# Add and GELU over 1024 x 4096: y loaded in three pieces in place of four, the adds dealt anew

## The chip, the core and the metric

One core of one Trainium2 chip. The metric is the device time of one execution in microseconds, the median of several; lower is better. A profile is taken of one further execution.

## The reference

```python
def reference(x, y):          # both 1024 x 4096, float32
    z = x + y
    return 0.5 * z * (1 + tanh(sqrt(2 / pi) * (z + 0.044715 * z ** 3)))
```

33.55 MB are read and 16.78 MB written.

## The kernel before

Eight rows of the input stand in each of the 128 partitions: 32768 columns. x is loaded into a tile z that holds everything and is worked on in place; y goes through two tiles of 8192 columns, so the third and fourth loads of y must wait until earlier columns have been added. A chunk is 2048 columns. z and y lie in SBUF, the core's on-chip memory. Each chunk takes four steps on three engines: an add (VectorE or GpSimd), the magnitude and the GELU of its negative (ScalarE, into PSUM, a second on-chip memory), and a close on VectorE, max(z, 0) + GELU(-|z|), which is the result.

```python
    YS = 8192; CH = 2048; PS = 2
    xloads = [16384, 16384]
    yloads = [8192, 8192, 8192, 8192]
    FIRST = 8
    stores = [16384, 10240, 6144]
    # chunk -> the close ahead of which VectorE's queue has this add; the other adds are GpSimd's
    by_dve = {0: 0, 2: 0, 4: 2, 6: 4, 8: 8, 12: 10}
    ...
    sp = [(load_y, 0), (load_x, 0), (load_y, 1), (load_x, 1), (load_y, 2), (load_y, 3)]
    sp += [(store, i) for i in range(len(stores))]
    pool = [(add, c) for c in range(C) if c not in by_dve]
    for c in range(C):
        dve += [(add, k) for k in sorted(by_dve) if by_dve[k] == c] + [(end, c)]
        acts += [(mag, c), (gelu, c)]
```

Each engine is given its instructions as one queue, and in the traces a ready instruction stands behind one that waits (VectorE's idle 4.12 us, below). All transfers are issued on one queue, in the order of `sp`, and are carried out by 16 DMA engines. A store waits for the close of the last chunk that it covers.

## Time and profile before

| | before |
|---|---|
| time, median | 120.04 us (3 runs) |
| span of the profiled run | 118.6 us |
| DMA share of the span | 98.6% |
| VectorE, ScalarE, GpSimd busy | 50%, 51%, 47% |
| second store issued | 96.34 us |

The groups of the page, by line, engine, operation and shape, with busy time, mean duration in ns, idle time before them and what ended it:

```profile
L149 POOL TENSOR_TENSOR z<-z,y 128x2048 f32<-128x2048 f32 x10 | 55.3, 5563 | 45.6 <-DMA z<-in_x_dram 31.1
L166 DVE SCALAR_TENSOR_TENSOR z<-z,w 128x2048 f32<-128x2048 f32 (+1 forms) x17 | 36.4, 2157 | 16.0 <-ACT w L157 16.0
L149 DVE TENSOR_TENSOR z<-z,y 128x2048 f32<-128x2048 f32 x6 | 24.0, 4009 | 30.3 <-DMA z<-in_x_dram 30.1
```

L149 is the add, on either engine; its means of 5.6 and 4.0 us include waiting for one another. L166 is the close.

### The profile page before, as it was taken

The numbers are of one execution on the slowest core, as the hardware profiler recorded it, in microseconds if no ns is written. First come the engines' busy times: TensorE is split into PE (matmuls) and PEld (weight loads), VectorE is DVE, ScalarE is ACT, GpSimd is POOL, SyncE is SP. The second block draws the span as 40 slices with busy tenths as digits, with TensorE's granted clock in tenths as the row PEclk, the third lists the DMA queues.
The fourth block names the chain that finished last, engine by engine and source line by source line (L and its number), as shares of the span: only waits on it lengthen the run. The fifth ranks groups of instructions, "written<-read, shape, count | busy, mean of one in ns | idle before, by whom it ended". The sixth has DMA issues, their size and how long they took to land.

```text
span 118.6 us, 160 instructions
## 1 busy us (share of the span) xinstructions
DVE 59.8 (50%) x24; ACT 60.8 (51%) x34; POOL 55.5 (47%) x14
## 2 busy tenths in 40 slices
DVE  0000000000399999699994594257999457742000
ACT  5000000000067979999379705797798999940000
POOL 0000000000399999997000029999999999100000
DMA  7989888998889988988899898998899889999996
GB/s 243 464 365 696 354 354 354 663 398 354 354 387 497 531 354 354 707 354 354 354 420 464 365 520 354 531 531 354 354 531 531 354 354 442 442 442 442 398 398 265
DMA packets 1296, 50.33 MB, mean 424 GB/s; under 512 B 144, under 2 KB 144, under 8 KB 144
## 3 DMA queue, kind: packets, MB, share of 16 engines
q1 hardware_dynamic: 1296, 50.33, 98.6%
HBM read 33.55 MB, written 16.78 MB: 424 GB/s over the span
## 4 chain that ended last, share of the span: by engine, by line
DMA 48%; POOL 34%; POOLq 4%; ACT 3%; DVE 2%; issue 0%; SPq 0%; DVEq 0%
POOL z L149 34%; DMA z<-in_x_dram 26%; DMA y<-in_y_dram 21%; POOLq L213 4%; DVE z L166 2%; ACT w L154 2%; ACT w L157 2%; SPq L132 0%; POOLq L149 0%; DVEq L166 0%
## 5 line engine op out<-in xcount | busy, mean ns | idle before, releaser
L149 POOL TENSOR_TENSOR z<-z,y 128x2048 f32<-128x2048 f32 x10 | 55.3, 5563 | 45.6 <-DMA z<-in_x_dram 31.1
L154 ACT ACTIVATE w<-z 128x2048 f32<-128x2048 f32 x16 | 30.1, 1880 | 42.5 <-DVE z L149 36.0
L166 DVE SCALAR_TENSOR_TENSOR z<-z,w 128x2048 f32<-128x2048 f32 (+1 forms) x17 | 36.4, 2157 | 16.0 <-ACT w L157 16.0
L149 DVE TENSOR_TENSOR z<-z,y 128x2048 f32<-128x2048 f32 x6 | 24.0, 4009 | 30.3 <-DMA z<-in_x_dram 30.1
L157 ACT ACTIVATE w<-w 128x2048 f32<-128x2048 f32 x16 | 29.8, 1862 | 0.5
L198 ACT ACT_TABLE_LOAD x1 | 1.3, 1283 | 1.3 <-PEq L230 1.3
L197 DVE MEMSET one<- 128x1 f32 x1 | 0.1, 59 | 1.3 <-PEq L230 1.3
L198 ACT ACTIVATE one<-one 128x1 f32<-128x1 f32 x1 | 0.2, 203 | 0.0
L230 POOL MEMSET const-float32-0.0<- 128x1 f32 x1 | 0.1, 98 | 0.2 <-issue 0.2
L230 POOL MEMSET const-bfloat16-1.0<- 128x1 bf16 x1 | 0.1, 101 | 0.0
L230 POOL MEMSET const-uint8-127<- 128x1 uint8 x1 | 0.1, 101 | 0.0
L230 POOL MEMSET const-float32-1.0<- 128x1 f32 x1 | 0.1, 98 | 0.0
## 6 DMA issues: line engine op xcount, KB each, us to landing
y<-in_y_dram SPq DMA_DIRECT2D x4, 4096.0 KB, 23.7
out_dram<-z SPq DMA_DIRECT2D x1, 5120.0 KB, 14.9
out_dram<-z SPq DMA_DIRECT2D x1, 3072.0 KB, 11.0
z<-in_x_dram SPq DMA_DIRECT2D x2, 44.9
out_dram<-z SPq DMA_DIRECT2D x1, 21.6
```

The costliest lines, as they stand in the source:

```text
L149: eng.tensor_add(out=zt[:, a:b], in0=zt[:, a:b], in1=yt[s][:, o : o + b - a])
L154: nc.scalar.activation(out=wt[c], in_=zt[:, a:b], func=act.Abs)
L157: nc.scalar.activation(out=wt[c], in_=wt[c], func=act.Gelu_apprx_tanh, scale=-1.0)
L166: ins = nc.vector.scalar_tensor_tensor(out=zt[:, a + o : a + o + n], in0=zt[:, a + o : a + o + n], scalar=0.0, in1=wt[c][:, o : o + n], op ...
L197: nc.vector.memset(one, 0.0)
L198: nc.scalar.activation(out=one, in_=one, func=act.Gelu_apprx_tanh)
L213: tc.compile()
L230: nc = _bacc.Bacc("TRN2", target_bir_lowering=False, num_devices=1)
```

## The change

Its intent: fewer and larger loads of y, with the third in place of the first columns of one larger tile; VectorE and GpSimd no longer fight for their shared port. A chunk boundary is put where the third load begins (column 20416), which makes a narrow chunk of 64 columns and turns chunk numbers from 10 on up by one.

```diff
-    YS = 8192
+    YS = 20416
-    yloads = [8192, 8192, 8192, 8192]
-    FIRST = 8
+    yloads = [8192, 12224, 12352]
+    FIRST = 9
-    xr, yr, sr, cr = (ranges(r) for r in (xloads, yloads, stores, [CH] * (TOT // CH)))
+    xr, yr, sr, cr = (ranges(r) for r in (xloads, yloads, stores, [CH] * 9 + [CH - 64, 64] + [CH] * 6))
-    by_dve = {0: 0, 2: 0, 4: 2, 6: 4, 8: 8, 12: 10}
+    by_dve = {0: 0, 2: 0, 4: 3, 6: 5, 10: 9, 11: 11, 12: 11, 14: 12, 16: 14}
+    turn = {1: 0, 13: 12, 15: 14}
...
+        if c in turn:
+            tc.add_manual_dep(ins.ins, adds[turn[c]].name, ...,
+                reason="the two engines take turns on their shared port")
...
-        store: lambda i: [(end, c) for c in over(cr, *sr[i])] + [(end, FIRST)],
+        store: lambda i: [(end, c) for c in over(cr, *sr[i])] + [(gelu, FIRST)],
```

(Cut: the first store now waits for the first half of a GELU, which is split in two, in place of half a close.)

## The prediction

> **What bounds the kernel now.** I read the page first, then the DMA queue's own waits, then the timeline of single stretches. On the page:
>
> ```profile
> span 118.6 us, 160 instructions
> DMA  7989888998889988988899898998899889999996
> q1 hardware_dynamic: 1296, 50.33, 98.6%
> DMA 48%; POOL 34%; POOLq 4%; ACT 3%; DVE 2%; issue 0%; SPq 0%; DVEq 0%
> ```
>
> The 16 DMA engines are busy for 98.6% of the span: 116.9 us of 118.6. Of the other 1.6 us, about 1.0 us lies before the first packet and 0.5 us after the last. The chain (last line) gives GpSimd 34%, but that is only the path followed back through the compute engines; while it adds, the queue goes on moving. So the kernel is bound by its 50.33 MB, and no compute engine can make it faster, only slower, by letting the queue run dry. What must be read is therefore how early each transfer joins the queue. The DMA issues, in the timeline of the sync engine:
>
> ```profile
> 44.68 0.33 SPq L132 DMA_DIRECT2D y<-in_y_dram  x1
> 57.94 0.33 SPq L132 DMA_DIRECT2D y<-in_y_dram  x1
> 77.61 0.35 SPq L136 DMA_DIRECT2D out_dram<-z  x1
> 96.34 0.34 SPq L136 DMA_DIRECT2D out_dram<-z  x1
> 107.56 0.33 SPq L136 DMA_DIRECT2D out_dram<-z  x1
> ```
>
> With the times from issue to landing (y: 12.0 to 39.8 us, x: 30.9 and 58.8, out: 21.6, 14.9, 11.0) the landings are y0 12.0, x0 31.35, y1 41.1, x1 60.4, y2 70.15, y3 79.85, and the stores 99.2, 111.25 and 118.55. The steps between them are 9.7 us for a load of 32 KB rows, 19.3 for 64 KB rows, 12.1 for 40 KB and 7.3 for 24 KB: proportional to bytes, without a gap. The engines run out of a transfer's packets about 0.5 to 0.8 us before it lands (the packets of the second store begin between 98.35 and 98.7, while the first lands at 99.2). So the margins are: first store issued at 77.61 for engines that come free from 79.07 on, 1.5 us; second store 96.34 for 98.35, 2.0 us; third 107.56 for 110.5, 2.9 us. These are the quantities that the change moves.
>
> The adds, by line, take 5563 ns on GpSimd and 4009 on VectorE on average, but single ones differ:
>
> ```profile
> 31.45 8.80 DVE L149 TENSOR_TENSOR z<-z,y 128x2048 f32<-128x2048 f32 x2 [30.06 <-DMA z<-in_x_dram]
> 31.49 6.61 POOL L149 TENSOR_TENSOR z<-z,y 128x2048 f32<-128x2048 f32 x1 [31.06 <-DMA z<-in_x_dram]
> 33.66 6.59 DVE L149 TENSOR_TENSOR z<-z,y 128x2048 f32<-128x2048 f32 x1
> 93.90 1.88 ACT L154 ACTIVATE w<-z 128x2048 f32<-128x2048 f32 x1
> 94.02 2.29 DVE L166 SCALAR_TENSOR_TENSOR z<-z,w 128x2048 f32<-128x2048 f32 x1 [1.64 <-ACT w L157]
> 95.81 1.86 ACT L157 ACTIVATE w<-w 128x2048 f32<-128x2048 f32 x1
> 97.58 1.88 ACT L154 ACTIVATE w<-z 128x2048 f32<-128x2048 f32 x1
> ```
>
> Alone, an add takes 2.29 us on VectorE and 4.50 on GpSimd. Here GpSimd's add waits 2.2 us for VectorE's first, and VectorE's second waits until GpSimd is through at 38.1, then works for 2.2. A chunk costs ScalarE 1.88 + 1.86, started every 3.68 us (93.90 to 97.58); the closing operation costs VectorE 2.29.
>
> **What the Trainium skill says.** "SBUF — State Buffer", Who interferes with whom: a VectorE instruction with two SBUF inputs and a GpSimd instruction that reads SBUF exclude each other for a whole instruction. The trace agrees (6.6 us in place of 4.5, and 6.6 in place of 2.3). "VectorE: DVE Perf Modes", the section on the TRN2 errata: an fp32 add of N columns takes (N+151)/0.96 ns; for 2048 that is 2.29 us, which the trace has, and for the new 64-column chunk 0.22 us, an estimate. "DMA: Bandwidth & Descriptors", Latency and other measured facts: about 0.6 us from a hardware-generated DMA to its first byte. In this trace the first packet starts 1.02 us after the first issue begins, 0.64 after it ends, which agrees if its 0.38 us are counted apart.
>
> **The change, part by part.**
>
> Loads. Four y loads become three, 32, 48.9 and 49.4 KB rows in place of four times 32. The bytes are the same. Per engine 32 row packets become 24. From the steps of 9.7 and 19.3 us, a 64 KB row takes twice a 32 KB row to within a few ns, so eight fewer packets and one fewer completion are worth 0 to 0.08 us; I take 0.03. New landings: y0 12.0 and x0 31.35 as before; y1 31.35 + 9.7 x 12224/8192 = 45.85; x1 + 19.35 = 65.2; y2 + 14.6 = 79.8; first store as before, engines free from 98.35 on. The floor does not move.
>
> Does y2 join in time? It overwrites columns used by adds 0 to 6. First add 0 and add 2 run back to back on VectorE (31.45 to 35.95), GpSimd does 1 and 3 until 40.4 and 44.85. ScalarE: chunk 1 from 40.4 to 44.2, chunk 2 to 47.85; VectorE closes chunk 2 at 50.15. GpSimd adds chunk 5 on y1's landing, 45.95 to 50.45. VectorE comes to add 4 at 50.1, waits until 50.45, ends at 52.6; chunk 4 leaves ScalarE at 56.4, is closed by 58.7, then add 6 runs to 60.9. y2 is issued at 60.9, engines come free from 64.4: 3.5 us of margin. In time.
>
> The first store. GpSimd adds chunks 8 and 9 from x1's landing: 65.3, 69.85, 74.2. ScalarE's magnitude of chunk 9 (1984 columns) ends at 76.05, the first half of the GELU about 1.0 us later; the store is issued at 77.1 for engines free from 79.05: 1.95 us in place of 1.5. In time.
>
> The second store. It needs chunks up to 13 (column 26624), and 11, 12 and 13 lie wholly in the last load. In the old kernel the last load brought only chunks 12 to 15, so the store waited for one chunk of it; now it waits for three. From y2's landing at 79.8: VectorE starts the 64-column add at 79.9 (0.24), then closes chunk 9 (1984 columns, 2.2) and 10 (0.24), both queued before add 11, then add 11: 79.9 + 0.24 + 2.2 + 0.24 + 2.29, less about 0.08 overlap at each of three joints, gives 84.65. ScalarE: three chunks at 3.68 from 84.7, the last ends at 84.7 + 2 x 3.68 + 3.77 = 95.8. Add 12 ends at 86.9 and add 13 on GpSimd at 91.4, neither in the way. VectorE closes chunk 13 from 95.9 to 98.2. **The second store is issued at about 98.25**, in place of 96.34, while the engines come free from 98.35 to 98.65. That is 0.1 us of margin where the first packet needs about 1.0. So the queue should run dry, for the first time, for 0.6 to 1.3 us: 98.25 + 1.0 = 99.25 against a mean of 98.55 for the first packets, more for the last engines, since at the start of the program the sixteen first packets began over 0.9 us. I take 0.85.
>
> The third store. Add 14 on VectorE waits for GpSimd and ends at 93.6, chunk 16 is added on VectorE by 100.4; ScalarE runs chunks 14, 15 and 16 from 95.75 to 106.9, the last close ends at 109.2. The second store's engines come free near 111.4. In time.
>
> Sum: -0.03 + 0.85 on 120.04 is 120.86; I say 120.85.
>
> **The rivals.** First, **nothing moves**: the restart is quicker than at program start, or end 13 comes half a microsecond earlier, and the time is 120.0 (119.95 to 120.15). For it: all first transfers of later DMAs in this trace follow without a gap with 1.5 us of margin, so the true need is known only to be under 1.5. Against it: 0.1 us is far below anything that this trace shows. Second, **y2 comes late**: if GpSimd's add 5 ended before VectorE asked at 50.1, GpSimd would take the port for add 7 and add 4 would end at 56.7; the chain behind it then puts y2's issue at 65.0, and the queue stands another 1.5 us, giving about 122.4. It needs an error of 0.35 us in my walk. Third, **the gain is real**: larger rows move faster, 119.9. The old trace's 64 KB rows are not faster per byte by more than 0.2%, so it can't be more than 0.1 us. Fourth, the restart is as slow as the program's start, where the first packets took up to twice their usual time; then the gap is 1.5 us and the time 121.5.
>
> **Range and chances.** A quarter of the weight lies on a gap under 0.5 us, most on 0.6 to 1.3, a little on two gaps. The range of 8 in 10 is 120.0 to 121.7. Faster by 2% would be 117.6, under the time of the bytes alone: 0.01. Slower by 2% is 122.4, only with both gaps: 0.05. The rest, 0.94, is within 2%.
>
> **What would show it.** Right: DMA share of the span falls to about 98%, with one gap, near 98.5 to 99.5, and y2's landing within 0.1 us of 79.8; the second store's issue at 98.2; VectorE's first two adds 2.29 us each, without a wait; GpSimd's adds 4.5 us nearly throughout. Wrong: the second store issued before 97.3 with no gap (then my walk from y2's landing is off), or issued at 98.2 and still no gap (then a transfer needs less lead than I think), or a gap at 64.5 (y2 late), or a changed packet time of the 48 KB rows.

## More of the kernel before

The spread is not small beside the effects: eleven runs of the kernel before, in one set of rounds, went from 119.99 to 120.64 us.

## The result, and the profile after

The changed kernel took **120.67 us** in the median (120.52 to 121.04, six runs), the kernel before in the same rounds 120.11. The ratio is 1.005, with a 95% interval of 1.0035 to 1.0065. Ratios here are the mean time of one kernel's runs over that of the other's of the same rounds, so not quite the ratio of the medians. The change makes the kernel slower by half a microsecond: within 2%, but clear of the scatter.

The lines of the page that answer to those shown of before:

```profile
span 119.2 us, 160 instructions
DMA  7989888988969989988896969998998889999796
q1 hardware_dynamic: 1152, 50.33, 98.3%
DMA 42%; ACT 26%; DVE 14%; POOL 5%; issue 4%; SPq 0%; DVEq 0%
L154 POOL TENSOR_TENSOR z<-z,y 128x2048 f32<-128x2048 f32 (+1 forms) x8 | 39.9, 5004 | 58.0 <-DVE z L154 48.6
L183 DVE SCALAR_TENSOR_TENSOR z<-z,w 128x2048 f32<-128x2048 f32 (+2 forms) x17 | 36.6, 2159 | 18.8 <-ACT w L176 18.7
L154 DVE TENSOR_TENSOR z<-z,y 128x2048 f32<-128x2048 f32 (+1 forms) x9 | 19.2, 2149 | 34.2 <-DMA z<-in_x_dram 30.1
```

The packets fell from 1296 to 1152 for the same bytes. The adds cost less on both engines: VectorE's from 24.0 to 19.2 us for nine in place of six, GpSimd's from 55.3 to 39.9 for eight in place of ten. So the compute side became cheaper, and the time rose: the engines were not the bound. The chain that ended last now has ScalarE with 26% in place of 3%, and the "issue" part rose from 0 to 4%; followed in order of time, 19.7 of its 30.9 us on ScalarE lie after the last load's landing, so the stores behind that load are the place to look. The timeline of the sync engine tells what (start, duration, what is issued):

```profile
60.97 0.33 SPq L137 DMA_DIRECT2D y<-in_y_dram  x1
77.01 0.35 SPq L141 DMA_DIRECT2D out_dram<-z  x1
98.37 0.34 SPq L141 DMA_DIRECT2D out_dram<-z  x1
109.45 0.33 SPq L141 DMA_DIRECT2D out_dram<-z  x1
```

The second store goes out at 98.37 in place of 96.34. In the kernel before, the DMA view of the stretch from 98.3 to 98.7 us shows the first store ending and the second beginning together:

```profile
DMA packets 32, 0.66 MB, mean 1639 GB/s; under 512 B 16, under 2 KB 16, under 8 KB 16
```

Sixteen of these packets are completions (under 512 B), one for each engine; the other sixteen are the second store's first rows of 40 KB. In the changed kernel it takes two stretches to find them, 98.4 to 99.1 and 99.1 to 99.5:

```profile
DMA packets 16, 0.00 MB, mean 0 GB/s; under 512 B 16, under 2 KB 16, under 8 KB 16
...
DMA packets 16, 0.66 MB, mean 1638 GB/s; under 512 B 0, under 2 KB 0, under 8 KB 0
```

Between them lies the gap. Packet by packet, the trace has the engines done with the first store from 98.50 to 99.03 us (mean 98.64), and the second store's first packets from 99.21 to 99.36 (mean 99.27): **0.63 us of idle per engine**. Before, the same change-over took 0.01. And why the store is late, on VectorE (the close is L183, the add L154) and ScalarE:

```profile
80.09 0.23 DVE L154 TENSOR_TENSOR z<-z,y 128x64 f32<-128x64 f32 x1 [4.12 <-DMA y<-in_y_dram]
80.23 2.35 DVE L183 SCALAR_TENSOR_TENSOR z<-z,w 128x1984 f32<-128x1984 f32 x2
82.50 4.49 DVE L154 TENSOR_TENSOR z<-z,y 128x2048 f32<-128x2048 f32 x2
...
93.65 4.69 DVE L183 SCALAR_TENSOR_TENSOR z<-z,w 128x2048 f32<-128x2048 f32 x2
94.09 1.86 ACT L176 ACTIVATE w<-w 128x2048 f32<-128x2048 f32 x1
98.37 0.34 SPq L141 DMA_DIRECT2D out_dram<-z  x1
```

VectorE stands idle for 4.12 us before the last load lands. The close of chunk 9, which needs nothing of that load, is ready for the last 2.1 us of this (its GELU ends at 78.01), but it is queued behind the 64-column add that waits for the load. Only after the closes of chunks 9 and 10 does VectorE add chunk 11, at 82.5. From there ScalarE needs three chunks, ending at 95.95, and the close of chunk 13 (the second of the two at 93.65) ends at 98.34.

### The profile page after: what moved, and what is told of

It reads as the page before. It is cut to its first block, busy times and chain, and to the rows that moved or that the text cites. A ratio compares the mean times of both kernels' runs of the same rounds, so it can differ in the third digit from the quotient of the medians.

```text
span 119.2 us, 160 instructions
## 1 busy us (share of the span) xinstructions
DVE 55.0 (46%) x27; ACT 61.1 (51%) x37; POOL 40.1 (34%) x12
## 2 busy tenths in 40 slices
DMA packets 1152, 50.33 MB, mean 422 GB/s; under 512 B 128, under 2 KB 128, under 8 KB 128
## 3 DMA queue, kind: packets, MB, share of 16 engines
q1 hardware_dynamic: 1152, 50.33, 98.3%
## 4 chain that ended last, share of the span: by engine, by line
DMA 42%; ACT 26%; DVE 14%; POOL 5%; issue 4%; SPq 0%; DVEq 0%
DMA z<-in_x_dram 26%; DMA y<-in_y_dram 16%; ACT w L169 14%; ACT w L176 12%; DVE z L154 8%; DVE z L183 6%; POOL z L154 5%; SPq L137 0%; DVEq L154 0%
## 5 line engine op out<-in xcount | busy, mean ns | idle before, releaser
L154 POOL TENSOR_TENSOR z<-z,y 128x2048 f32<-128x2048 f32 (+1 forms) x8 | 39.9, 5004 | 58.0 <-DVE z L154 48.6
L169 ACT ACTIVATE w<-z 128x2048 f32<-128x2048 f32 (+2 forms) x17 | 30.2, 1779 | 44.1 <-DVE z L154 39.4
L183 DVE SCALAR_TENSOR_TENSOR z<-z,w 128x2048 f32<-128x2048 f32 (+2 forms) x17 | 36.6, 2159 | 18.8 <-ACT w L176 18.7
L154 DVE TENSOR_TENSOR z<-z,y 128x2048 f32<-128x2048 f32 (+1 forms) x9 | 19.2, 2149 | 34.2 <-DMA z<-in_x_dram 30.1
L176 ACT ACTIVATE w<-w 128x2048 f32<-128x2048 f32 (+2 forms) x18 | 30.1, 1672 | 0.6
## 6 DMA issues: line engine op xcount, KB each, us to landing
y<-in_y_dram SPq DMA_DIRECT2D x1, 6176.0 KB, 19.1
```

What stands on the lines that cost most here:

```text
L154: ins = eng.tensor_add(out=zt[:, a:b], in0=zt[:, a:b], in1=yt[:, o : o + b - a])
L169: nc.scalar.activation(out=wt[c], in_=zt[:, a:b], func=act.Abs)
L176: ins = nc.scalar.activation(out=w, in_=w, func=act.Gelu_apprx_tanh, scale=-1.0)
L183: nc.vector.scalar_tensor_tensor(out=zt[:, a:b], in0=zt[:, a:b], scalar=0.0, in1=wt[c], op0=alu.max, op1=alu.add,)
```

## The experiments

Twelve runs were made; all gave the right result. "Gap" is the mean over the engines between the last packet of the first store and the first of the second, from the trace's packets. "Before" is the kernel before in the same rounds.

| run | second store issued | gap | time, median | before | ratio (95%) |
|---|---|---|---|---|---|
| the change | 98.37 | 0.63 | 120.67 | 120.11 | 1.0050 (1.0035 to 1.0065) |
| after_again | 98.34 | 0.54 | 120.61 | 120.08 | 1.0038 (1.0026 to 1.0051) |
| e1_close_first | 96.54 | 0.01 | 120.33 | 120.11 | 1.0014 (0.9996 to 1.0031) |
| e1_again | 96.64 | 0.01 | 120.18 | 120.08 | 1.0002 (0.9988 to 1.0016) |
| e2_later_store | 102.64 | 5.03 | 124.92 | 120.11 | 1.0397 (1.037 to 1.0424) |
| e3_no_turns | 103.00 | 5.36 | 125.40 | 120.11 | 1.0437 (1.041 to 1.0464) |
| e4_four_loads | 96.21 | 0.01 | 120.08 | 120.11 | 1.0016 (0.9983 to 1.0048) |
| e4_again | 96.25 | 0.01 | 120.53 | 120.11 | 1.0040 (1.0007 to 1.0074) |
| e5_lead_one | 97.26 | 0.00 | 120.60 | 120.08 | 1.0038 (1.0025 to 1.0052) |
| e6_lead_half | 97.83 | 0.11 | 120.61 | 120.08 | 1.0042 (1.0026 to 1.0058) |
| e7_early_load | 96.69 | 0.00 | 120.46 | 120.13 | 1.0020 (1.0005 to 1.0035) |
| e8_lead_clean | 97.47 | 0.02 | 120.19 | 120.13 | 1.0013 (0.9994 to 1.0033) |
| e9_more_instructions | 96.42 | 0.00 | 120.51 | 120.13 | 1.0032 (1.0018 to 1.0046) |

**e1_close_first and e1_again: the same kernel with the late store mended.** My theory: the loss is the dry queue at the second store. The rival: the loads themselves cost it. The close of chunk 9 needs nothing of the last load, so it goes ahead of the adds that do:

```diff
-    by_dve = {..., 10: 9, 11: 11, 12: 11, 14: 12, 16: 14}
+    by_dve = {..., 10: 10, 11: 10, 12: 10, 14: 12, 16: 14}
```

> The changed kernel, with VectorE's queue turned round in one place: the close of chunk 9 stands ahead of the adds that wait for the last load, and the adds of chunks 11 and 12 ahead of the close of chunk 10. Theory (the loss is the dry queue at the second store): add 11 ends at 82.6 us in place of 84.8, the second store is issued at about 96.2 in place of 98.37, 2.3 us before the first engine comes free, no gap is left, and the time is 119.95 to 120.15, a ratio to the kernel before of 0.999 to 1.001. Rival A (48 KB rows or the three loads themselves cost the half microsecond): the time stays at 120.5 to 120.7. Rival B (the restart costs more than the lead explains, and part of the loss is elsewhere): between the two, about 120.3.

The first measurement had a median of 120.33, between the two theories and where rival B had put it, with single runs from 119.98 to 120.59, so I ran it again beside the changed kernel:

> The changed kernel once more, beside the others on one chip. Theory: 120.5 to 120.8, the second store issued at 98.1 to 98.4, its first packets 0.85 to 1.0 us later, and a gap of about 0.6 us.

> The reordered kernel again, since its first measurement had a median of 120.33 with a spread of 0.6 us and did not separate it from either kernel. Its profile had no gap, but one of the 16 DMA engines finished the first load 0.4 us behind the others and stayed behind to the end. Theory (the gap was the loss; what is left is the scatter of the slowest engine, which the kernel before has too): no gap, 119.95 to 120.35, and 0.3 to 0.6 us faster than after_again. Rival (three loads or 48 KB rows cost something): it stays 0.2 us or more above the kernel before.

The repeat of the change gave 120.61, the reordered kernel 120.18 and the kernel before 120.08. The reordered kernel's timeline and the DMA view of 98.6 to 99.2 us in its second profile:

```profile
78.49 2.22 DVE L183 SCALAR_TENSOR_TENSOR z<-z,w 128x1984 f32<-128x1984 f32 x1 [2.13 <-ACT w L176]
80.63 4.62 DVE L154 TENSOR_TENSOR z<-z,y 128x64 f32<-128x64 f32 x3
...
96.64 0.34 SPq L141 DMA_DIRECT2D out_dram<-z  x1
...
DMA packets 32, 0.66 MB, mean 1092 GB/s; under 512 B 16, under 2 KB 16, under 8 KB 16
```

The close of chunk 9 has moved into the idle time, the three adds follow one another, the store is issued 1.7 us earlier, and completions and first rows stand in one stretch again. No gap is left, and 0.43 us of the 0.53 us that separate the two kernels in these rounds are back. (By the first measurement it was 0.34 of 0.56, with the change measured in other rounds.) So the gap is shown to be most of the loss. Whether the last tenth is real is not: the intervals of both measurements include 1.

**e2_later_store: the same cost, eight times as large.** The second store covers one chunk more.

```diff
-    stores = [16384, 10240, 6144]
+    stores = [16384, 12288, 4096]
```

> The changed kernel with the second store widened by one chunk (48 KB rows, the third store 16 KB), so that it waits for chunk 14. In the changed kernel's trace that chunk is closed at 102.74. Theory (each microsecond that the second store comes late is a microsecond of dry queue): first packets near 103.65 where the engines are free at 98.6, a gap of 5.0 in place of 0.6, and the time is 120.67 + 4.4 = 125.0. Rival (the gap is only partly exposed, since later stores catch up): clearly under 124.

It took 124.92 us, 4.25 more than the change, against 4.4 expected. Issue and first packets (103.3 to 103.7 us):

```profile
102.64 0.34 SPq L141 DMA_DIRECT2D out_dram<-z  x1
...
DMA packets 16, 0.79 MB, mean 1966 GB/s; under 512 B 0, under 2 KB 0, under 8 KB 0
```

The gap of 5.03 us raises the time by 4.81 over the kernel before. With e3 (5.36 and 5.29) and the change itself (0.63 and 0.56) that makes three sizes of gap: the time rises by nearly the whole of it, each time by 0.07 to 0.22 us less. What the small rest is, is not shown. In the profiles the last packet ends 0.78, 5.06 and 5.41 us later than in the kernel before, so no less than the gap, and the span ends 0.38 us after it in place of 0.51.

**e3_no_turns: the waits that make the engines take turns.** The three added waits are taken out (`turn = {}`); no data depends on them.

> The changed kernel without the three added waits that make the two engines take turns. Theory (the port goes to whoever asks first and the queue in the port alternates): on the last load's landing GpSimd adds chunk 13 first, 80.3 to 84.8, VectorE's add 11 waits to 86.9, GpSimd goes on with add 15 until 91.3, VectorE's add 12 ends at 93.5; the second store goes out near 103.4 and the time is about 125.7, 5 us slower than the changed kernel. Rival (the lock alternates anyhow, so the waits are superfluous): within 0.3 us of the changed kernel, 120.4 to 121.0.

125.40 us, against 125.7 expected and 120.67 with the turns. GpSimd's and VectorE's adds after the last load:

```profile
79.89 11.06 POOL L154 TENSOR_TENSOR z<-z,y 128x2048 f32<-128x2048 f32 x2 [5.77 <-DMA y<-in_y_dram]
...
82.25 10.85 DVE L154 TENSOR_TENSOR z<-z,y 128x2048 f32<-128x2048 f32 x2
...
103.00 0.34 SPq L141 DMA_DIRECT2D out_dram<-z  x1
```

Two adds of VectorE took 10.85 us where the change has 4.49. GpSimd takes the port at 79.89 for a chunk that is not wanted yet, and once both ask, they alternate, whole instruction by whole instruction. So within this dealing the turns are worth 4.7 us; the rival, that they are superfluous, falls. They save no transfer time: they keep the wrong chunk from being added first, and the second store from being later still.

**e4_four_loads and e4_again: is it the number of loads?** The kernel of e1 with the last load in two halves, the first of which can be issued at 44.8.

```diff
-    yloads = [8192, 12224, 12352]
+    yloads = [8192, 12224, 6176, 6176]
```

> The kernel of e1_close_first with the last load of y cut into two of 24.7 KB rows, so four loads again. Theory (the transfer time is a matter of bytes; a packet and a completion more cost some ns): the same time as e1_close_first within 0.1 us. Rival (fewer and larger rows are what the change gains): 0.1 to 0.3 us slower than e1_close_first. If the queue had a margin problem at the last load, landing earlier in two halves would show here as a gain, which the theory does not expect, since e1_close_first has no gap.

> The reordered kernel with the last load in two halves, again: its first measurement had one run at 121.18 among six and a median of 120.08. The kernels with three loads and no gap had medians of 120.33, 120.18, 120.46 and 120.19 against 120.11, 120.08, 120.13 and 120.13 of the kernel before. Theory A (three loads cost 0.1 to 0.2 us through slow packets, of which e4's first profile had none): a median of 119.95 to 120.15, no run of slow packets in the profile. Theory B (it is scatter of the transfers, whatever the loads): a median of 120.1 to 120.4 and slow packets among the loads.

The medians were 120.08 and 120.53, 0.25 under and 0.35 over those of e1 in the same order, so both sets missed what was expected of them. In the second set three runs lay from 120.00 to 120.20 and three from 120.86 to 121.26, and one of the first six was at 121.18. Both profiles fell among the quick ones and show no gap and, after the first load, no slow packet among the loads, so what the slow ones are is unknown, and neither theory is confirmed. What stands is that the quick runs of four loads (119.91 to 120.43, picked after the fact) are no slower than those of three or of the kernel before: the larger rows bring nothing that the times can show.

**e5_lead_one, e6_lead_half, e8_lead_clean: how much lead a store needs.** In e5 and e6 the close of chunk 13 is cut into 16 and 24 parts, which delays the store.

```diff
+        for n in [128] * 16 if c == 13 else [b - a]:     # e6: [64] * 16 + [128] * 8
```

> The reordered kernel with the close of chunk 13 cut into 16 parts of 128 columns, so that the second store goes out about 1.0 us later, near 97.2, some 1.2 us before the first engine comes free. Theory (a transfer needs 0.85 us from issue to first packet, and no more): no gap, the time of e1_again within 0.1 us. Rival (a running queue needs the lead of the program's start, 1.0 to 1.9 us): a gap for a part of the engines, 0.2 to 0.6 us slower.

> The same with 24 parts (16 of 64 columns, 8 of 128), so that the second store goes out near 97.85, about 0.55 us before the first engine comes free. Theory: first packets near 98.7 where the engines come free between 98.3 and 98.7, so a gap of 0.1 to 0.4 us by engine; because the last engine to come free sets the end and it waits least, the time rises by 0.0 to 0.25 us over e1_again. Rival (lead as at the program's start): 0.6 us or more.

Both took 120.6, half a microsecond over the kernel before, and so against my expectation. But in the trace e5 has no gap: its store is issued at 97.26, and the packets follow at once from 98.52. e6's store is issued at 97.83, its first packets begin at 98.68, the mean gap is 0.11. The lead was as expected and the time was not, so the cuts must have cost something else. The pages of both have a line that those of all the runs above lack, a packet of 8 KB on the instruction queue; in e6 it comes at 98.6 and a 40 KB packet that starts just after takes 1.87 us in place of 1.51. It looks as if the 15 and 23 added instructions made the core fetch instructions in the middle of the run, on one of the 16 DMA engines. That is not the whole of it: in their profiles the last engine ends only 0.17 us (e5) and 0.33 us (e6) after the next one, and e5's last load also had nine first packets that were 0.05 to 0.35 us too long. So I delayed the store with a single instruction more, starting from e7 (below), by closing 480 columns of chunk 9 before the last load's landing and 1504 after the first add behind it:

> e7_early_load with the close of chunk 9 in two parts, 480 columns before the last load's landing and 1504 after the add of chunk 10, so that the second store goes out near 97.5, 0.8 us before the first engine comes free, with one instruction more instead of the 15 and 23 of e5 and e6, whose profiles show an instruction fetch of 0.35 us on one DMA engine. Theory (0.85 us from issue to first packet is all that a store needs, and e5 and e6 were slow because of the fetch): gaps of at most 0.1 us, no packet on the instruction queue, the time of e7_early_load within 0.1 us. Rival (a store that goes out late costs even without a gap): 0.3 us or more slower than e7_early_load.

```profile
97.47 0.34 SPq L141 DMA_DIRECT2D out_dram<-z  x1
...
DMA packets 32, 0.66 MB, mean 936 GB/s; under 512 B 16, under 2 KB 16, under 8 KB 16
```

The store goes out 0.87 us before the first engine is done (98.34), completions and first rows stand in one stretch (98.2 to 98.9), there is no packet on the instruction queue, and the median is 120.19, faster than its sibling e7 by 0.27 where I had expected at most 0.1. The rival, that a late store costs even without a gap, falls. As to the lead: where the engines stood idle (the change, after_again, e2, e3), the sixteen first packets came 0.84 to 0.99 us after the issue. A lead of 0.87 us just about covers that; it left 0.02 us of gap in the mean and about 0.13 at most. (e6, 0.61 us ahead of the first engine, left 0.11 us.)

**e9_more_instructions: the fetch by itself.** The kernel of e7 with the close of chunk 0, which has much time around it, in 16 parts.

> e7_early_load with the close of chunk 0 cut into 16 parts, long before any store: 15 more VectorE instructions, nothing else moved that a transfer waits for. Theory (the extra instructions make an instruction fetch fall into the run, and it takes one DMA engine 0.35 us): one packet on the instruction queue, one data packet 0.35 us too long, and the time 0.2 to 0.45 us above e7_early_load, since the slowest engine sets the end. Rival (e5 and e6 were slow through the late store): the time of e7_early_load.

The page has the packet again:

```profile
q1 hardware_dynamic: 1152, 50.33, 98.2%
q14 instruction: 1, 0.01, 0.0%
```

The fetch took 0.31 us, from 111.67, and the data packet after it, at 111.98 us, took 0.37 us too long. Fifteen of the engines end by 118.15 us, the one with that packet at 118.71: it alone sets the end. In this profile the fetch put off the end by 0.56 us. The times don't show it as I had expected: 120.51 is 0.32 over e8 but only 0.05 over e7, with which I had said I would compare it, so by that measure the rival's outcome came; e7 was itself slow, with slow packets in its profile. All three kernels with 15 or more added instructions show the fetch and no other does. How much of e5's and e6's half microsecond it is, is not shown.

**e7_early_load: does the last load go out too late?** In the traces with three loads, some first packets of the last load took 0.05 to 0.35 us too long. Its issue, at 61, is 3.5 us before its first packet. I exchanged two adds so that it goes out at 57.

```diff
-    by_dve = {..., 4: 3, 6: 5, ...}
+    by_dve = {..., 4: 3, 7: 6, ...}
```

> The reordered kernel (e1) with chunks 6 and 7 exchanged between the engines: GpSimd adds 6 right after 5, VectorE adds 7 later. The last load, which waits for add 6, should go out near 57.1 in place of 61.2, 7.4 us ahead of its first packets in place of 3.4. Theory (a load issued only 3.4 us ahead starts with slow packets: in all eight runs with three loads some first packets of the last load took 0.05 to 0.35 us too long, in none of the two with four): these packets take their usual 1.825 us, the slowest engine ends the load within 0.45 us of the fastest, and the time falls from about 120.2 to 120.0 to 120.1, level with the kernel before. Rival (scatter, unrelated to when the load is issued): some first packets of the last load are slow here too and the time stays at 120.2 to 120.3.

A miss. The time was 120.46, no lower than e1's. Its first packets were still up to 0.12 us too long, and moreover the 64 KB rows of the second x load took 2.47 us on average in place of 2.42, in nearly all engines. In e8, with the same loads, there was hardly any of that. So when the last load is issued is not what makes these packets slow, or not alone. Such stretches came and went between profiles of nearly the same kernel.

## Why the prediction was right

The time on record was 120.85 and the measured one 120.67, of which 0.56 us are the change against 0.81 foretold (the kernel before read 0.07 us higher in these rounds). Point by point:

- **What bounds the kernel.** Right: cheaper adds bought nothing, and the time moved with the gap in the DMA queue alone, over three sizes of gap.
- **Loads.** The issue of the last load was foretold for 60.9 and came at 60.97, its landing for 79.8 and came at 80.07 (issue and 19.1 us), outside the 0.1 us that the prediction allowed it. The gain of 0.03 us from fewer packets is too small to be seen in the times. By the packets' median durations it is 0.06 us: an engine's y rows take 8 x (1.213 + 1.806 + 1.825) us in place of 32 x 1.213; slow packets outweighed that.
- **First and third store.** Foretold for 77.1 and 109.2, seen at 77.01 and 109.45, both in time.
- **Second store.** Foretold for 98.25, seen at 98.37; e1 shows that this lateness is most of the loss.
- **The size of the gap.** The term that was off: 0.85 us against 0.63. The first packet's mean time was right (99.25 foretold, 99.27 seen). But I had added to it for a start spread over 0.9 us, as at the program's start, and the sixteen first packets began within 0.15 us; and the engines came free at 98.64 in the mean, not at 98.55, in part because first packets of the last load were slow (1.88 us in the mean where 1.825 is usual). The median time then rose by a little less than the gap.
- **The rivals.** "Nothing moves" fell: 0.1 us of margin was too little, and e8 shows that 0.87 would have been all but enough. "y2 comes late" did not happen: add 4 took the port as walked. "The gain is real" fell with e1 and e4, which have no gap and are no faster than the kernel before. The slow restart fell: the second store's first packets took 1.535 us on average, where this size took 1.515 before, and its eight rows lost 0.09 us together. (Nor were the first packets of the program up to twice the usual, as this rival had it: in the trace of before the longest took 2.135 us for 1.213, 1.76 times.)
- **GpSimd's adds** were foretold to take 4.5 us nearly throughout; two of eight took 6.5, waiting on the port.
- The two first adds of VectorE took 2.29 us each without a wait, as foretold; GpSimd's first then waits for both:

```profile
31.47 4.49 DVE L154 TENSOR_TENSOR z<-z,y 128x2048 f32<-128x2048 f32 x2 [30.08 <-DMA z<-in_x_dram]
...
33.84 10.95 POOL L154 TENSOR_TENSOR z<-z,y 128x2048 f32<-128x2048 f32 x2 [33.41 <-DVE z L154]
```

**What stays open.** The kernels without a gap (e8's of 0.02 counted in) had medians of 120.08 to 120.60 against 120.08 to 120.13 of the kernel before. Whether 0.1 us of that belongs to the new loads, why e5 and e7 took 0.3 to 0.5 us more without a gap, and why some runs of e4 took a whole microsecond more, these runs don't settle. No version here beats the kernel before.

## What to carry to other kernels

When the DMA share is 98%, read the margins, not the busy times: for every transfer, how long before the queue runs dry it is issued. A larger last load gives the work behind it less time: here it put three chunks in place of one between that load's landing and the second store, and the margin went from 2 us to 0.1. Look in each in-order queue for work that stands behind a wait it doesn't need; moving one close ahead of the waiting adds, and two adds ahead of another close, took the store 1.7 us forward.

## What the Trainium skill lacked or had wrong

- "DMA: Bandwidth & Descriptors", Latency and other measured facts: the page doesn't say from where its 0.6 us to the first byte are counted; here they fit from the end of the issue (0.50 to 0.65 us for the sixteen engines). From the start of the issue, in the middle of a run, the first packets came after 0.84 to 0.99 us. Nor does it say what lead keeps a running queue from a gap: 1.26 us did, 0.87 left 0.02 us of gap, 0.61 left 0.11, 0.13 left 0.63.
- "SBUF — State Buffer", Who interferes with whom: it says that whoever issues first holds the port for its whole instruction and the other waits. It doesn't say who is next: in e3 the two engines alternated, so that two adds of VectorE took 10.85 us.
- "Runtime: NRT & Kernel Launch", Instruction fetch mechanics: it calls the cost of crossing a block boundary mostly hidden. In the profile of e9, bound by its transfers, it was not: with 15 more instructions came one 8 KB packet of 0.31 us on the instruction queue, the next data packet took 0.37 us longer, and its engine ended 0.56 us after the others.
- No page has that equal packets differ between executions: 64 KB rows took 2.42 us on average in most profiles and 2.47 in e7's second x load.
